# A hybrid recurrent decoder step on one core: the RWKV-7 scan in three products per chunk

## The chip, the cores and the metric

One Trainium2 chip, of which one core is used. The metric is the device time of one execution in microseconds (us). An execution computes one step of a two-layer decoder trunk for 512 prompt rows and 8 x 4 sample rows, 544 columns in all.

## The reference

```python
# layer 0: RG-LRU and RWKV-7 side by side; layer 1: HGRN2; a SwiGLU FFN after each, RMSNorm everywhere
p = rmsnorm(x) @ w_in_ab                     # 1024 -> 1024 (RG-LRU) + 1792 (RWKV-7)
m = pf + (shifted - pf) * mu                 # r, k, v and three low-rank inputs
decay = exp(-exp(-softplus(-(w0 + tanh(xw) @ w2)) - 0.5));  a = sigmoid(a0 + xa @ a2)
kk = (k * k_k) / |k * k_k|;  k = k * (1 + (a - 1) * k_a)
def _rwkv_step(S, inp):                      # 8 heads, S is 64 x 64 [value, key]
    sk = einsum('bhvk,bhk->bhv', S, kk_t)
    S = S * w_t - sk (kk_t * a_t) + v_t k_t
    return S, einsum('bhvk,bhk->bhv', S, r_t)
y = concat(gelu(gate) * rg_lru(conv(u)), (groupnorm(o) + bonus) * g) @ w_out_ab
```

The outputs are y for both groups and all the new states, in float32.

## The kernel before

Everything lies transposed: features on partitions, the 544 columns along the free dimension. A projection (`dense_steps`) makes one block of 128 outputs in two halves of 272 columns; each half is 24 matmuls (8 blocks of the inner dimension, each as high times high, high times low, low times high in fp32r). A block is called a column here: 48 matmuls, two weight loads of 256 KB on SP's queue, a rounding of each on ScalarE (wh, L198) and a difference on VectorE or GpSimd (wl, L201). Three wh and three wl buffers hold weights. The result is taken from its bank by VectorE (X, L465), and `proj_end` mixes it with its shifted self (d on GpSimd, L471; then L473).

The RWKV-7 recurrence is done in chunks of 32 steps, 16 chunks, 8 heads. Heads are numbered by p (0 to 3, a block of 128 features) and par (which half of the block). `mixer0` stages it:

1. **Projections ahead**: the low-rank block and k blocks.
2. **Features** (`FEAT` lists the steps): `front` normalises kappa, `back` makes the decay products eb, KB (key and kappa parts divided by the decay, 64 columns a chunk) and A (kappa times decay), `couple` multiplies A with KB to get the coupling of the steps of a chunk (NTt, and masked into AN), `alphas` transposes A into AN on TensorE.
3. **Inverse**: the coupling goes through DRAM (nd_p) to a layout of 128 (head, chunk) pairs; VectorE inverts the two diagonal 16 x 16 blocks of each 32 x 32 triangle in 15 steps (L670, L672); ScalarE transposes (Zc); both go through DRAM (y_p, z_p) to Yt and Zt.
4. **Fixed order** (`MID` lists the steps): a and b start a half of a `keys`, r a `receptance`, v is a value projection, g the gate's; capitals are their second parts (transposes into TM, `scores` and bonus), x a transpose of values to DRAM (vT). From here on `in_order = "all"`: every matmul of the steps waits for the one before it in program order.
5. **Scan**: `PLAN` interleaves the chunks (c), the sample group's steps (s), group norms (g, h) and the output projection's start (l). `join` completes the inverse of four chunks (32 x 32 tiles), `fold` multiplies AN by it on TensorE and copies the result to wa. Then for each chunk a first product (wa with Z, where Z holds the 64 state rows, the values and the corrections of a chunk), two copies into Z, and a second product (TM with Z) to which the decayed state is added for the next Z; `outputs` reads Z too. Between the products `fill(n)` issues n matmuls of the RG-LRU branch's projections; `HOP` gives the two counts.

What no fixed order binds is placed by a planner at build time, which simulates the queues with its own costs; `high_priority` moves work ahead. All DMAs are issued on SP's queue in order. The engines run their queues in order.

The lines that matter in profiles: L167 all matmuls of `mm`, known by tile (acc projections, scps scores, wyps fold, ch the two products, ops outputs, jps join, knps and kkps the kappa norm, sps the sample's corrections); L596 to L599 the kappa product and its small copies; L612 the mask of AN; L670, L672 inverse; L686 loads of Yt and Zt; L730 r times decay; L784 and L782 copies of the first product (and of wa); L788 the load of values; L861 the decayed state; L876 the next state.

## Time and profile before

| | us |
|---|---|
| median of three runs | 1554.47 (1553.48 to 1555.07) |
| the profiled execution | 1550.75 |
| its span, first to last instruction | 1549.0 |
| TensorE busy in the span | 1475.5 (95%) |
| VectorE busy | 841.7 (54%) |
| ScalarE busy | 565.9 (37%) |
| GpSimd busy | 422.2 (27%) |

The profile is one execution. Busy times of stretches give engines in the order TensorE, its weight loads, VectorE, ScalarE, GpSimd, then the granted TensorE clock as a share of full speed, the share of the DMA engines and GB/s. A row of a group has the line, the engine, the operation, output<-inputs, shapes and count, then busy us and mean ns of one, then the idle time just before with what ended it. A row of a timeline has start, length, engine, line, operation. A row of the chain of waits has start, length and what held the end. Matmuls overlap, so a mean of one is a latency; the pace is read from many in a row. A matmul in float32 shows as two instructions.

The mixer of layer 0 takes the first 351 us; the features lie at about 59 to 105, the fixed order at 105 to 182, the chunks at 195 to 336.

### The profile page before, as it was taken

Reading aid. Unit: us, or ns where it says so; the run is one execution under the profiler, and the core shown is the slowest. Engines: PE = TensorE matmul, PEld = TensorE weight load, DVE = VectorE, ACT = ScalarE, POOL = GpSimd, SP = SyncE. Lnnn points to the kernel's source line nnn. Section 1 sums busy time; section 2 is a strip of 40 time slices with the busy share of each in tenths; the row PEclk is TensorE's granted clock in tenths of the full one; section 3 lists DMA queues with packets and bytes.
Section 4 is the critical chain, followed back from the end, with each engine's and each line's share of the span. In section 5 each row is a group of like instructions: output and inputs, shape, how many; then the busy total and the mean of one; then the engine's idle time right before and its main releaser. Section 6 shows DMA issues by size and latency. Waiting matters only on the chain.

```text
span 1549.0 us, 33454 instructions
## 1 busy us (share of the span) xinstructions
PE 1475.5 (95%) x13888; PEld 1425.7 (92%) x13888; DVE 841.7 (54%) x1560; ACT 565.9 (37%) x1030; POOL 422.2 (27%) x545
## 2 busy tenths in 40 slices
PE   6669999879999999999999999999999999999997
PEld 6658888759999999999999999999999999999997
DVE  7646535785544344434576767666674443444444
ACT  5644234473433223222353333333453322332224
POOL 4535624553111011001124434444431100110010
PEclk9869988889999999999999999999999999999999
DMA  4115401122222322322231222322332223223221
GB/s 160 52 31 137 124 25 34 43 94 87 82 95 84 90 89 89 90 83 95 81 122 67 85 85 86 101 96 84 103 123 89 95 81 92 89 89 89 83 75 59
DMA packets 91480, 133.79 MB, mean 86 GB/s; under 512 B 28448, under 2 KB 34336, under 8 KB 91200
## 3 DMA queue, kind: packets, MB, share of 16 engines
q1 hardware_dynamic: 91328, 131.65, 27.2%
q8 instruction: 109, 1.79, 0.5%
q14 instruction: 43, 0.35, 0.1%
HBM read 120.60 MB, written 11.02 MB: 85 GB/s over the span
## 4 chain that ended last, share of the span: by engine, by line
PE 85%; DVE 6%; ACT 3%; issue 2%; DMA 2%; POOL 1%; SPq 0%; DVEq 0%; POOLq 0%; ACTq 0%
PE acc L167 74%; PE lv L167 2%; PE ops L167 1%; PE wyps L167 1%; PE ch L167 1%; DMA wd<-down 1%; PE ds L167 0%; POOL wl L201 0%; PE tr L1528 0%; PE nps L167 0%; PE scps L167 0%; DVE Pd L670 0%; DVE cf L1038 0%; DVE Y L672 0%; PE opsm L167 0%
## 5 line engine op out<-in xcount | busy, mean ns | idle before, releaser
L167 PE MATMUL acc<-xg,wh 128*128 128x272 f32 x4544 | 881.8, 292 | 13.5 <-ACT xg L258 6.5
L167 PEld LDWEIGHTS acc<-xg,wh 128*128 128x128 f32 x4544 | 718.2, 190 | 21.4 <-ACT xg L258 6.5
L167 PE MATMUL acc<-xg,wl 128*128 128x272 f32 x2272 | 651.2, 292 | 1.1 <-DVE wl L201 0.7
L198 ACT ACTIVATE wh<-wf 128x512 fp32r<-128x512 f32 (+1 forms) x404 | 250.7, 621 | 632.0 <-PE acc L167 538.3
L167 PEld LDWEIGHTS acc<-xg,wl 128*128 128x128 f32 x2272 | 427.4, 190 | 5.0 <-DVE wl L201 1.4
L201 DVE TENSOR_TENSOR wl<-wf,wh 128x512 fp32r<-128x512 f32 (+1 forms) x373 | 266.7, 716 | 190.1 <-ACT wh L198 164.0
L1232 POOL TENSOR_TENSOR S<-S,rstd 128x272 f32<-128x272 f32 x88 | 74.5, 847 | 645.6 <-ACT S L1231 645.6
L167 PE MATMUL acc<-h,wh 128*128 128x272 f32 x1280 | 236.9, 288 | 0.0
L167 PEld LDWEIGHTS acc<-h,wh 128*128 128x128 f32 x1280 | 198.0, 188 | 0.0
L167 PE MATMUL acc<-h,wl 128*128 128x272 f32 x640 | 176.7, 287 | 0.0
L167 PEld LDWEIGHTS acc<-h,wl 128*128 128x128 f32 x640 | 118.1, 188 | 0.0
L1235 DVE TENSOR_TENSOR hh<-acc,S 128x272 f32<-128x272 f32 x88 | 38.9, 442 | 125.6 <-PE acc L167 123.8
L167 PE MATMUL acc<-cat,wh 128*128 128x272 f32 (+2 forms) x512 | 99.4, 294 | 5.1 <-ACT wh L198 5.1
L167 PEld LDWEIGHTS acc<-cat,wh 128*128 128x128 f32 x512 | 82.2, 193 | 5.7 <-ACT wh L198 5.3
L1231 ACT ACTIVATE S<-t 128x272 f32<-128x272 f32 x88 | 37.8, 431 | 124.0 <-DVE t L1230 124.0
L1252 DVE TENSOR_TENSOR x<-acc,x 128x272 f32<-128x272 f32 x80 | 35.1, 439 | 83.5 <-PE acc L167 83.1
L167 PE MATMUL acc<-cat,wl 128*128 128x272 f32 (+2 forms) x256 | 73.8, 295 | 3.9 <-POOL wl L201 3.9
L1230 DVE TENSOR_TENSOR t<-acc,rstd 128x272 f32<-128x272 f32 x88 | 38.8, 442 | 71.2 <-PE acc L167 71.1
L276 POOL TENSOR_TENSOR ssq<-ssq,sq 128x544 f32<-128x544 f32 x33 | 46.6, 1411 | 87.7 <-ACT sq L275 87.3
L1502 POOL TENSOR_TENSOR K<-K,G 128x256 f32<-128x256 f32 (+1 forms) x48 | 39.6, 824 | 77.5 <-PE lv L167 77.5
L167 PEld LDWEIGHTS acc<-cat,wl 128*128 128x128 f32 x256 | 48.7, 192 | 4.5 <-POOL wl L201 4.5
L201 POOL TENSOR_TENSOR wl<-wf,wh 128x512 fp32r<-128x512 f32 x31 | 42.6, 1378 | 25.9 <-ACT wh L198 24.0
(355 smaller groups left out, 1549.6 us busy)
## 6 DMA issues: line engine op xcount, KB each, us to landing
wf<-gate SPq DMA_DIRECT2D x88, 256.0 KB, 2.6
wf<-up SPq DMA_DIRECT2D x88, 256.0 KB, 2.7
wf<-down SPq DMA_DIRECT2D x72, 256.0 KB, 2.7
wf<-w_in_c SPq DMA_DIRECT2D x64, 256.0 KB, 2.5
wf<-w_in_ab SPq DMA_DIRECT2D x44, 256.0 KB, 2.7
x<-xT SPq DMA_DIRECT2D x16, 272.0 KB, 4.4
wf<-w_out_ab SPq DMA_DIRECT2D x16, 256.0 KB, 2.5
S<-hS SPq DMA_DIRECT2D x8, 512.0 KB, 3.8
```

The costliest lines, as they stand in the source:

```text
L167: return self.seq(self.nc.tensor.matmul(out, lhsT, rhs, start=start, stop=stop, skip_group_check=True), chain)
L198: nc.scalar.activation(wh[:, :n], wf[:, :n], AF.Copy)
L201: eng.tensor_tensor(wl[:, :n], wf[:, :n], wh[:, :n].bitcast(F32), OP.subtract)
L276: eng.tensor_tensor(self.ssq, self.ssq, t, OP.add)
L1230: nc.vector.tensor_tensor(t[:, c], ps, rs()[:, c], OP.mult)
L1231: nc.scalar.activation(S[:, c], t[:, c], AF.Silu)
L1232: nc.gpsimd.tensor_tensor(S[:, c], S[:, c], rs()[:, c], OP.mult)
L1235: nc.vector.tensor_tensor(hh[:, c], ps, S[:, c], OP.mult)
L1252: nc.vector.tensor_tensor(x[:, c], ps, x[:, c], OP.add)
L1502: PTT(kv[:, :, 0], kv[:, :, 0], g2[:, :, 1, None].to_broadcast([128, m, b]), OP.mult)
```

## The change

The first product of a chunk is split. Before, the inverse was folded into the kappa rows ahead of the chunks (fold, 16 matmul calls for two chunks at a time) and one product gave the corrections. Now the first product gives the right-hand side (kappa rows with Z) in quarter q of the partitions for each head pair, VectorE copies it (rhs), a second product multiplies it by the inverse, with the heads on the four diagonal 32 x 32 quarters of the array, four copies on VectorE put the corrections into Z, and the state's product follows. `HOP` has three counts.

For that the rows of kappa, r and the scores share one array W (64 columns a chunk: 32 for kappa, 32 for r, the sample as chunk 16), so `scores` makes both masked parts in one matmul a chunk, in three tiles; the order of corrections and values in Z's rows and in KB's columns depends on p's parity (`quad`, VS, US). AN, A2, As, Ws, tmask, `alphas` and `fold` go. `couple` handles two p at once with half the columns, and writes nd_p in eight DMAs of 32 partitions; Yt and Zt are loaded in 16 DMAs instead of 8; the values of a chunk in four DMAs instead of two. The pools of W and TM are part of m0, the inverse's tiles are opened after the features, and the scan's pool follows where eb and KB lay.

The value projections stand first in `MID`, and the fixed order begins only at the step r3, so that v0 to v3, a3 and b3, a1 and A3 are placed by the planner.

```diff
--- before.py
+++ after.py
+FREE = 'r3'
-MID = 'a3 v0 A3 b3 v2 B3 a1 v3 A1 b1 r3 B1 a2 v1 R3 A2 b2 r0 x B2 x a0 r1 x R0 A0 x b0 r2 x R1 B0 g R2'
+MID = 'v0 v2 v3 a3 v1 A3 b3 a1 r3 B3 A1 b1 a2 r0 R3 B1 A2 x b2 a0 x r1 x B2 R0 A0 x b0 r2 x R1 B0 g R2'
-FEAT = 'f0 b0 f2 f1 b1 b2 f3 n0 n1 b3 n2 n3'
+FEAT = 'f0 b0 f2 f1 b1 b2 n0 f3 b3 n1'
-HOP = (11, 11)
+HOP = (8, 7, 7)
...
-        AN = m0.tile([128, 4, 4, 256], F32, name="AN")
-        nc.gpsimd.memset(AN[:, :, :, 96:192], 0.0)
+        W = [[m0.tile([128, NC1, 64], F32, name=f"W{par}{p}") for p in range(4)] for par in range(2)]
+        TM = [m0.tile([128, NC1, 64], F32, name=f"TM{p}") for p in range(4)]
...
-        v_rows = (slice(64, 96), slice(0, 32))
-        s_rows = (slice(96, 128), slice(32, 64))
+        VS, US = [slice(CH, 64), slice(0, CH)] * 2, [slice(0, CH), slice(CH, 64)] * 2
+        def quad(par, e):
+            return slice(64 - 64 * par + 32 * e, 96 - 64 * par + 32 * e)
...
         def scores(p):
-            ps = mps("scps").rearrange("p (c t) -> p c t", t=CH)
-            for c in range(NCH):
+            for c0, cn in ((0, 8), (8, 8), (16, 1)):
+                ps = self.ms.tile([128, 8, 64], F32, tag="m", name="scps")
+                for c in range(c0, c0 + cn):
+                    for par in range(2):
+                        r = par_rows[par]
+                        self.mm(ps[sc_rows[par], c - c0], KB[p][r, c], W[par][p][r, c])
                 for par in range(2):
-                    r = par_rows[par]
-                    self.mm(ps[sc_rows[par], c], KB[p][r, c], W[par][r, c, p])
-            for par in range(2):
-                sr = sc_rows[par]
-                TT(W[par][sr, :, p], ps[sr], smask[sr, 0, None, CH:].to_broadcast([64, NCH, CH]), OP.mult)
...
-        def alphas(p):
-            ps = mps("atps").rearrange("p (g k) -> p g k", k=128)
-            for g in range(4):
-                nc.tensor.transpose(ps[:, g], A2[p][:, 4 * g:4 * g + 4].rearrange("p c t -> p (c t)"), ident)
-            an = AN[:, :, p]
-            out = bass.AP(tensor=an.tensor, offset=an.offset, ap=[an.ap[0], an.ap[1], [192, 2], [1, 64]])
-            ACT(out, ps.rearrange("p g (q k) -> p g q k", q=2), AF.Copy)
+                    sr = sc_rows[par]
+                    TT(W[par][p][sr, c0:c0 + cn], ps[sr, 0:cn],
+                       smask[sr, p % 2, c0 // 16, None, :].to_broadcast([64, cn, 64]), OP.mult)
...
-            STT(KB[p][:, :, CH:], chunks(ta), -0.5, chunks(emb), op0=OP.mult, op1=OP.mult)
-            al = A2[p]
-            E(f"al{p % 2}")(al, chunks(kap), chunks(eb[p][:, 0:NT]), OP.mult)
-            nc.gpsimd.tensor_copy(al[:, 0:NCH, 0:1], kap[:, 0:SEQ:CH][:, :, None])
-            nc.gpsimd.tensor_copy(al[:, NCH, 0:CH:NS], kap[:, SEQ::NS])
-            nc.gpsimd.tensor_copy(As[:, p], al[:, NCH])
-
-        def couple(p):
-            ps = [self.ms.tile([128, 4, 64], F32, tag="m", name="ndps") for _ in range(2)]
+            STT(KB[p][:, :, US[p]], chunks(ta), -0.5, chunks(emb), op0=OP.mult, op1=OP.mult)
+            for par in range(2):
+                r = par_rows[par]
+                al = W[par][p][r, :, 0:CH]
+                E(f"al{par}")(al, chunks(kap[r]), chunks(eb[p][r, 0:NT]), OP.mult)
+                nc.gpsimd.tensor_copy(al[:, 0:NCH, 0:1], kap[r, 0:SEQ:CH][:, :, None])
+                nc.gpsimd.tensor_copy(al[:, NCH, 0:CH:NS], kap[r, SEQ::NS])
+
+        def couple(s):
+            ps = mps("ndps").rearrange("p (c t) -> p c t", t=CH)
             for c in range(NCH):
+                for e in range(2):
+                    p = 2 * s + e
+                    for par in range(2):
+                        r = par_rows[par]
+                        self.mm(ps[quad(par, e), c], W[par][p][r, c, 0:CH], KB[p][r, c, US[p]])
+            ACT(NTt[:, s], ps, AF.Copy)
+            for q in range(4):
+                r = slice(32 * q, 32 * q + 32)
+                nc.sync.dma_start(nd_p[4 * s + q].rearrange("c t i -> t c i"), NTt[r, s])
-                    self.mm(ps[par][quarter(c), c // 4], A2[p][r, c], KB[p][r, c])
-            for par in range(2):
-                nt = NTt[:, :, 4 * par + p]
-                ACT(nt, ps[par][:, :, CH:], AF.Copy)
-                nc.sync.dma_start(nd_p[4 * par + p].rearrange("(g c) t i -> (c t) g i", c=4), nt)
-            for par in range(2):
-                TT(AN[:, :, p, 64 + 64 * par:96 + 64 * par], ps[par][:, :, 0:CH],
-                   tmask[:, None, :].to_broadcast([128, 4, CH]), OP.mult)
...
-                alphas(p)
...
-        wt = self.open("wt")
-        W = [wt.tile([128, NCH, 4, CH], F32, name=f"W{par}") for par in range(2)]
-        Ws = [wt.tile([128, 4, 64], F32, name=f"Ws{par}") for par in range(2)]
-        TM = [wt.tile([128, NC1, 64], F32, name=f"TM{p}") for p in range(4)]
+        iv = self.open("inv", side="right")
...
-            for g in range(4):
+            for h in range(8):
+                r = slice(32 * (h % 4), 32 * (h % 4) + 32)
                 for zt, dr in ((Yt, y_p), (Zt, z_p)):
-                    nc.sync.dma_start(zt[:, g], dr.rearrange("h (g c) i t -> g (c i) h t", c=4)[g])
+                    nc.sync.dma_start(zt[r, :, h // 4], dr[h].rearrange("c i t -> i c t"))
...
-                E(f"w{par}")(W[par][r, :, p], chunks(rm[r, :SEQ]), chunks(eb[p][r, 1:1 + SEQ]), OP.mult)
-                nc.gpsimd.tensor_tensor(Ws[par][r, p, CH:], rm[r, SEQ:], eb[p][r, 1 + SEQ:], OP.mult)
+                E(f"w{par}")(W[par][p][r, :, CH:], chunks(rm[r]), chunks(eb[p][r, 1:]), OP.mult)
...
-        self.in_order = "all"
         parts = {}
         values = values_out()
         for e in MID.split():
+            if e == FREE:
+                self.in_order = "all"
...
-        both = chp.tile([128, 2, 4, 64], F32, name="ch")
-        chain = [both[:, i] for i in range(2)]
+        chain = chp.tile([128, 512], F32, name="ch")
+        cr, cu = (chain[:, 128 * i:128 * i + 128].rearrange("p (s v) -> p s v", v=64) for i in range(2))
+        cs = chain[:, 256:512].rearrange("p (a v) -> p a v", v=64)
...
         def load_v(c, zc):
             for par in range(2):
-                nc.sync.dma_start(zc[par][v_rows[par]], vT[CH * c:CH * c + CH, :, par_rows[par]])
-
+                for e in range(2):
+                    nc.sync.dma_start(zc[par][quad(par, 1 - e), e::2], vT[CH * c:CH * c + CH, e::2, par_rows[par]])
+        heads = [(p, par) for p in range(4) for par in range(2)]
...
+            ps = ms.tile([128, 4, 2, HB], F32, tag="m", name="jps")
+            for s in range(2):
+                for c in range(4 * g, 4 * g + 4):
+                    for q in (slice(32 * i, 32 * i + 32) for i in range(4)):
+                        if part:
+                            self.mm(ps[q, c % 4, s], Zt[q, c, s], joined[g][q, c % 4, s])
+                        else:
+                            self.mm(ps[q, c % 4, s], NTt[q, s, c], Yt[q, c, s, HB:])
...
-        def fold(g, cs):
-            pss = [self.acc.tile([128, 2, 4, CH], F32, tag="acc", name="wyps", bufs=3) for _ in cs]
-            for par in range(2):
-                for p in range(4):
-                    for ps, c in zip(pss, cs):
-                        q = quarter(c)
-                        self.mm(ps[:, par, p], AN[q, g, p, 128 * par:128 * par + 128],
-                                Yt[q, g, 4 * par + p], chain=True)
-            for ps, c in zip(pss, cs):
-                wa = z.tile([128, 2, 4, CH], F32, tag="wa", name="wa", bufs=6)
-                copy(c % 2, wa, ps)
-                folded[4 * g + c] = wa
...
-                    self.mm(ops[quarter(p), c % 4, par], W[par][:, c, p], zc[par][:, p], chain=True)
+                    self.mm(ops[quarter(p), c % 4, par], W[par][p][:, c, CH:], zc[par][:, p], chain=True)
...
-            with first():
-                fold(0, (0, 1))
-                fold(0, (2, 3))
             for c in range(NCH):
+                rhs = z.tile([128, 2, 64], F32, tag="rhs", name="rhs", bufs=2)
                 with first():
-                    for p in range(4):
-                        for par in range(2):
-                            self.mm(chain[0][s_rows[par], p], folded[c][:, par, p], zc[par][:, p], chain=True)
-                    for par in range(2):
-                        copy(par, zc[par][s_rows[par]], chain[0][s_rows[par]])
+                    for p, par in heads:
+                        self.mm(cr[quad(par, p % 2), p // 2], W[par][p][:, c, 0:CH], zc[par][:, p], chain=True)
+                    nc.vector.tensor_copy(rhs, cr)
...
-                if c < 12:
-                    with first():
-                        if c % 4 > 1:
-                            fold(c // 4 + 1, ((0, 1), (2, 3))[c % 2])
-                        else:
-                            join(c // 4 + 1, c % 4)
+                    if c < 12 and c % 4 < 2:
+                        join(c // 4 + 1, c % 4)
                 self.fill(HOP[0])
                 with first():
-                    for p in range(4):
+                    for p, par in heads:
+                        q = quad(par, p % 2)
+                        self.mm(cu[q, p // 2], Yt[q, c, p // 2], rhs[q, p // 2], chain=True)
+                    for e in range(2):
                         for par in range(2):
-                            sr = sc_rows[par]
-                            self.mm(chain[1][par_rows[par], p], TM[p][sr, c], zc[par][sr, p], chain=True)
+                            q = quad(par, e)
+                            nc.vector.tensor_copy(zc[par][q, e::2], cu[q])
+                self.fill(HOP[1])
+                with first():
+                    for p, par in heads:
+                        sr = sc_rows[par]
+                        self.mm(cs[par_rows[par], p], TM[p][sr, c], zc[par][sr, p], chain=True)
                     for par in range(2):
                         r = par_rows[par]
-                        TT(zn[par][r], chain[1][r], sp[r], OP.add)
+                        TT(zn[par][r], cs[r], sp[r], OP.add)
...
-                self.fill(HOP[1])
+                self.fill(HOP[2])
                 yield
```

More of the change, by code (lines that the diff above doesn't have):

```diff
@@ L106, in rows, with pair @@
         return np.concatenate([top, bot, top, bot], 0)
-    c["smask"] = np.stack([rows(strict, incl), rows(strict * same, incl * same)], 1)
-    c["tmask"] = np.tile(strict.T, (4, 1))
+    def pair(flip):
+        m = np.stack([rows(strict, incl), rows(strict * same, incl * same)], 1)
+        return m.reshape(2, 2, 32, 2, 64)[:, ::-1].reshape(128, 2, 64) if flip else m
+    c["smask"] = np.stack([pair(True), pair(False)], 1)
     c["upper"] = np.tile((np.arange(CH) < CH // 2)[:, None], (4, 1)).astype(np.float32)
@@ L504, in mixer0 @@
         L = f.tile([128, NT], F32, name="L")
-        A2 = [f.tile([128, NC1, CH], F32, name=f"A2{p}") for p in range(4)]
-        As = m0.tile([128, 4, CH], F32, name="As")
         def tmp(name, bufs=2):
@@ L614, in couple @@
[L614 to L621 removed]
+                    self.mm(ps[q_rows[par]], KB[p][r, NCH, US[p]], W[par][p][r, NCH, 0:CH])
@@ L623, in mixer0 @@
+                ACT(ss, ps, AF.Copy)
+                for par in range(2):
+                    nc.sync.dma_start(nd_s[4 * par + p], ss[q_rows[par]])
         kaps = [None] * 4
@@ L985, in sample @@
                 for p in range(4):
-                    self.mm(sps[s_rows[par], p], Yts[q_rows[par], p], rhs[q_rows[par], p])
-                ACT(zc[par][s_rows[par]], sps[s_rows[par]], AF.Copy)
+                    self.mm(sps[quad(par, p % 2), p], Yts[q_rows[par], p], rhs[q_rows[par], p])
+                for e in range(2):
+                    ACT(zc[par][quad(par, e), e::2], sps[quad(par, e), e::2], AF.Copy)
             yield
@@ L1136, in mixer0 @@
         nc.sync.dma_start(self.o["h_o"], h_sb)
-        self.close("rg", "scan", "wt", "m0", "ms_s", "ops0", "chain")
+        self.close("rg", "scan", "m0", "ms_s", "ops0", "chain")
         self.ms = self.open("ms", bufs=4, space=PSUM)
```

53 lines of the change are left out of this document (14 added, 39 removed).

## The prediction

> **What bounds the kernel now.** I read first the chain of waits of the page, then busy times by stretch, the acc groups of one stretch, and the timelines of TensorE (PE) and SyncE's queue (SPq) around the seams.
>
> ```profile
> PE 85%; DVE 6%; ACT 3%; issue 2%; DMA 2%; POOL 1%; SPq 0%; DVEq 0%; POOLq 0%; ACTq 0%
> ```
> ```profile
> core 0: us, PE busy (x) PEld busy (x) DVE busy (x) ACT busy (x) POOL busy (x), PEclk, DMA share, GB/s
> 59.50:105.00 45.50, 20.62 (x347) 15.52 (x346) 27.83 (x42) 21.90 (x45) 19.45 (x30) 0.64 0.10 22
> 128.00:182.00 54.00, 50.65 (x590) 48.06 (x588) 31.05 (x58) 21.60 (x45) 34.69 (x61) 1.00 0.50 133
> 195.40:240.80 45.40, 41.68 (x778) 36.93 (x776) 20.63 (x46) 17.42 (x30) 14.75 (x22) 0.88 0.12 33
> 283.80:330.50 46.70, 41.43 (x479) 34.09 (x479) 37.06 (x79) 23.64 (x43) 28.94 (x31) 0.89 0.16 51
> ```
>
> TensorE sets the end nearly everywhere, but the change touches only the first 351 us, and there the share hides two limits. In 59.5 to 105 (the features) TensorE works 20.6 of 45.5 us at a granted clock of 0.64: it waits for short vector steps. From 105 to 182 (the phase in fixed order) it is full. In the scan it is nearly full until about 284; after that VectorE is busy 79% of the time.
>
> ```profile
> L167 PE MATMUL acc<-xg,wl x1: 375/375/375, 59.3 to 59.3; 128*128 128x272 f32 x1
> ```
> ```profile
> L167 PE MATMUL acc<-xg,wh 128*128 128x272 f32 x276 | 53.5, 292 | 1.8 <-ACT wh L198 1.8
> L167 PE MATMUL acc<-xg,wl 128*128 128x272 f32 x138 | 40.1, 291 | 1.1 <-DVE wl L201 0.7 <-POOL wl L201 0.4
> ```
> ```profile
> 148.19 5.98 PE acc L167 x48
> ```
>
> The first row holds the only projection matmul in the features. The second pair is 105 to 182: 414 matmuls, eight columns of 48 and the 30 of the first fill. The order has nine columns (four v, four r, the gate), so v0 ran before 59.5 and v1, v2, v3 stand after 105, although they need only xg and weights: A3 stands ahead of v2 in the fixed order, and A3 needs KB3, one of the last products of the features. A column costs 5.98 us.
>
> **Value projections.** Put outside the order, v1 to v3 can fill the 24.9 idle us: 3 x 5.98 = **-17.9** from the full stretch. Each brings vector work into the features.
>
> ```profile
> L201 DVE TENSOR_TENSOR wl<-wf,wh 128x512 fp32r<-128x512 f32 x84 | 61.3, 731 | 50.2 <-ACT wh L198 44.0 <-PE acc L167 2.9
> L465 DVE TENSOR_TENSOR X<-acc,rstd 128x272 f32<-128x272 f32 x28 | 11.8, 435 | 7.3 <-PE acc L167 5.3 <-ACT rstd L308 1.9
> L473 DVE SCALAR_TENSOR_TENSOR v<-d,vec,X 128x544 f32<-128x544 f32 x4 | 3.1, 779 | 0.4 <-POOL d L472 0.4
> L596 DVE TENSOR_TENSOR A<-kap,eb 128x544 f32<-128x544 f32 x2 | 1.4, 725 | 1.4 <-ACT eb L584 1.4
> L612 DVE TENSOR_TENSOR AN<-ndps,tmask 128x128 f32<-128x128 f32 x8 | 1.9, 284 | 4.4 <-ACT NTt L609 4.4
> L596 POOL TENSOR_TENSOR A<-kap,eb 128x544 f32<-128x544 f32 x2 | 2.7, 1344 | 0.0
> L598 POOL COPY A<-kap 128x8 f32<-128x8 f32 x4 | 2.0, 499 | 0.0
> L471 POOL TENSOR_TENSOR d<-X 128x544 f32<-128x544 f32 x14 | 17.4, 1242 | 0.0
> ```
>
> VectorE: 6 x 0.435 + 4 wl x 0.731 (a third goes to POOL) + 3 x 0.779 = 7.9. The kappa product is now one VectorE and one POOL instruction of 64 partitions for each p instead of one of either: +2 x 0.725, and the eight masks of AN go, -2.3. Together +7.0 on an engine with 17.7 us idle. POOL takes three d (3.7), two more kappa products (2.7) and about four more small copies net (2.0) into 26 idle us. The chain here alternates between engines, so an added operation costs only where it stands ahead of a due one: bounds 0 and 7.0, I take **+3**.
>
> Against this stands the clock. The same eight matmuls take
>
> ```profile
> 48.53 0.93 PE knps L167 x8
> 65.62 2.18 PE knps L167 x8
> 84.24 2.18 PE knps L167 x8
> ```
>
> before and inside the features, twice on the chain: **-2.5** if the columns keep the clock up, else 0. The 16 transposes of alphas and their copies also go; I count nothing, since vector steps set this stretch. Were they bare, it would be about another microsecond for each p.
>
> **Scores, couple, inverse.**
> ```profile
> 137.04 2.05 PE L167 MATMUL scps<-W,KB 64*64 64x32 f32 x64 [1.32 <-POOL W L730]
> ```
>
> Scores keep their number of matmuls, with 64 columns moving instead of 32 and three tiles to mask instead of two: between nothing and 0.65 us per r (2.05 for 64 now; 2.7 at the pace of the 64x64 products below, 16 in 0.68). I take **+1** for all four. The added masks lie beside projections. POOL's product of r with eb must precede each scores; one stall of 1.32 is there today, and the cover stays one column: **+1**, bounds 0 and 4. Couple does the same number of matmuls with half the columns and its first half moves ahead of f3: 0, hidden by vector steps as above.
>
> ```profile
> 127.40 0.22 DVE Pd L670
> ```
> ```profile
> 130.50 2.93 SPq L686 DMA_DIRECT2D Yt<-y_p  x4
> 133.53 2.52 SPq L686 DMA_DIRECT2D Zt<-z_p  x4
> ```
> ```profile
> 182.03 0.73 PE L167 MATMUL jps<-Yt,NTt 32*32 32x16 f32 x64
> ```
>
> The inverse ends at 127.6, its loads are issued by 136 and wanted at 182. After: nd_p is still eight DMAs, now bunched four by four (about 2 us later), and Yt and Zt take 16 issues in place of 8; at 2.93/4 each that is at most 6 us more on SPq, ahead of weight loads. The loads land near 147; the first join would come near 167. I count **0**, covered by the r projections; without the cover, a microsecond for each that they are late. The scan's tiles now lie where eb and KB were, so Z's first writes wait for r2's product; the gate's column (5.98) stands behind that one, and without it up to the 4.14 of a Z load (below) would be bare.
>
> Features and fixed order: -17.9 + 3 - 2.5 + 1 + 1 = **-15**.
>
> **Start of the scan.**
>
> ```profile
> 186.25 1.33 PE L167 MATMUL wyps<-Yt,AN 32*128 32x32 f32 x12
> 188.31 2.34 PE L167 MATMUL wyps<-Yt,AN 32*128 32x32 f32 x20 [0.72 <-issue]
> 191.81 3.62 PE L167 MATMUL wyps<-Yt,AN 32*128 32x32 f32 x32 [1.16 <-DVE wa L784]
> ```
> ```profile
> 181.88 4.14 DMA Z<-vT
> ```
> ```profile
> L788 SPq DMA_DIRECT2D Z<-vT x18: 538/548/690, 181.1 to 236.4; - x18
> ```
>
> The first fold stands bare from 186.25 to 195.4 (191.81 + 3.62), its second half behind a copy that VectorE does late. Without a fold the first product can go at once: -9.1. It needs its values, landed at 186.0 with no slack now. Each slot takes four DMAs instead of two, the sample's too: four more issues of 0.55 ahead of the first slot's last, +2.2. **-7**, bounds -9 and -3.
>
> **Each chunk.**
>
> ```profile
> 204.53 0.66 PE L167 MATMUL ch<-Z,wa 128*32 128x64 f32 x15
> 207.00 0.41 PE L167 MATMUL acc<-xg,wh 128*128 128x272 f32 x2
> 207.34 0.68 PE L167 MATMUL ch<-Z,TM 64*64 64x64 f32 x16
> 207.95 0.43 PE L167 MATMUL ops<-Z,W 128*32 128x64 f32 x16
> 211.58 1.97 PE L167 MATMUL wyps<-Yt,AN 32*128 32x32 f32 x32
> 238.28 1.06 PE L167 MATMUL sps<-rhss,Yts 32*32 32x64 f32 x8
> 284.71 3.93 PE L167 MATMUL wyps<-Yt,AN 32*128 32x32 f32 x32
> ```
> ```profile
> L876 DVE TENSOR_TENSOR Z<-ch,sp 64x256 f32<-64x256 f32 x32 | 13.5, 421 | 14.0 <-PE ch L167 9.0 <-ACT gg L1074 2.2 <-ACT wh L198 1.9
> L784 DVE COPY Z<-ch 32x256 f32<-32x256 f32 x16 | 6.9, 430 | 12.9 <-PE ch L167 12.6
> ```
>
> TensorE: six folds go (five like 1.97, one of 3.93): -13.7. The first product uses four column groups instead of two, as ops does: 0.66 to 0.43, -3.7 over 16 (bounds 0 and -3.7). The new product of 32x32 tiles isn't in the trace in this arrangement: below, ops with 0.43; above, two of sps, whose eight share one tile, 2.1. Here neighbours never share a tile, as in ops and in jps (64 in 0.73): 0.45, +7.2 (bounds 6.9 and 34, for the range half of that). Sum -10.2; the 22 fills a chunk stay.
>
> Latency: the copy of rhs (128 elements a partition, as L612: 0.28) hides under eight fill matmuls (8 x 0.125). Behind the new product stand four copies, 4 x 0.28 and a start of 0.15 = 1.27, against seven fills, 0.88: bare 0.4 in each chunk, **+7** with the gaps between copies. Behind the waiting state's product queue, in order, the outputs, the fill, the sample's products and the next chunk; the two sums into the next slot wait for it. VectorE gets 5 x 0.28 and loses one Z copy (0.43) and half a copy of a fold, of the same size (0.21): +0.76 a chunk. Up to 284 it is idle enough; in the 5.5 chunks at 79% I take it whole: **+4.2** (bounds 0 and 12). ScalarE loses its copies, which bounds nothing.
>
> Loop: -10.2 + 7 + 4.2 = **+1**, bounds -8 and +20.
>
> The Trainium skill, TensorEngine Tiling (Array Packing), Key Properties, says that a change of tiling mode drains the engine, which speaks against one more product between fills. In the rows at 207 the 64x64 product starts about 0.09 us later than another matmul of the fill would have, so two more changes in 16 chunks would add 2.9 us, and the whole would come to -18.
>
> **Sum.** -15 - 7 + 1 = -21. The profiled execution took 1550.75 (span 1549.0): 1529.7. The median shown, 1554.47, lies 3.7 higher, so on its scale **1533**.
>
> **Rivals.** *More moves.* The order now begins at r3, and nothing precedes r3's matmuls: 24.9 idle us hold a fourth column. Against it: r3's buffers and the planner. Another -6, with no stretch of the features -3 more, and -2 in the loop: 1522.
>
> *They don't move.* Three weight buffers and in-order ACT and DVE queues may keep the columns behind the features, or they stretch that chain as much as they free. For it: the chain there lives on DVE and ACT, as the columns do; against: 17.7 idle us. Features and order give -1, the rest -6: 1547.
>
> *The third hop decides (slower).* Place: VectorE's queue in the scan. Both new waits are on VectorE, whose other operations, 0.4 to 0.8 us in the rows above, run to their end. If each of the two waits for one like L473 (0.78), a chunk gets 1.56 us longer, 25 in all: -21 + 25 = +4, 1558. It decides from 21/16 = 1.3 us a chunk. For it: 79% busy after 284, and a fold's copy is late behind VectorE at 191.8; against: half idle until 284, and a hop to ScalarE goes.
>
> **Chances.** Forecast 0.47, more moves 0.20, not moved 0.16, third hop 0.17. A measurement here tells 0.2% (3 us) from nothing. Of "not moved" 0.03 and of the third hop 0.02 fall within that: faster 0.80, same 0.05, slower 0.15. The forecast's own range is 1522 to 1545; with the bounds above and most of the rivals, 1511 to 1555.
>
> **What would show it.** Right: some 140 acc matmuls between 59 and 105 at a clock near 1; the first join near 167; under 1.5 us from the new product to the state's product; no wyps. Wrong: features ending after 110, join waiting for Yt, chunks over 9 us, TensorE idle behind the four copies for more than a microsecond.

## The result, and the profile after

The changed kernel takes **1541.53 us** (median of four runs, 1540.40 to 1541.86) against 1553.97 (1549.24 to 1555.07) for the kernel before on the same chip: a ratio of 0.9924, 95% interval 0.9903 to 0.9946. That is 12.4 us by medians; the profiled executions, 1550.75 and 1541.22, lie 9.5 apart, and the sum of the prediction (-21) is made on that scale; less than half of it came. One of the four runs with the fills on VectorE below was in the slow state (1789 us) and is left out of its figures.

The chain of waits of the page after is almost the one before:

```profile
PE 84%; DVE 7%; ACT 3%; issue 2%; DMA 2%; POOL 1%; SPq 1%; DVEq 0%; POOLq 0%; ACTq 0%
```

Busy times by stretch, in the columns of the prediction, with the seams where this trace has them:

```profile
59.50:107.00 47.50, 40.33 (x532) 35.44 (x530) 40.34 (x53) 24.66 (x44) 32.86 (x48) 0.92 0.19 57
107.00:128.00 21.00, 11.22 (x74) 10.20 (x73) 13.19 (x35) 6.27 (x17) 9.20 (x16) 0.61 0.23 55
128.00:176.00 48.00, 42.30 (x526) 39.00 (x526) 30.41 (x59) 18.58 (x40) 24.21 (x44) 0.93 0.44 116
```

The features, 20.6 us of TensorE work at a clock of 0.64 before, are now nearly full: 40.33 of 47.5 us at 0.92. The hole has moved. It stands now in the first 21 us of the fixed order, where TensorE works 11.22 us at 0.61; before, the same length of this phase was full (20.11 us from 105 to 126, at 0.97).

The table puts seams of several kernels side by side; the runs are those of the next section. Each is read from TensorE's timeline: the end of the last couple's product (ndps), the first join (jps), the first product of chunks 0, 1 and 15, and the first product of the norm that follows the mixer (nps). What lies behind nps takes 1145 to 1146 us in all of them. The first product of the kappa norm (kkps), ahead of all these seams, starts at 43.1 to 44.9 us, so a difference of under 2 us in the place of a single seam says nothing; lengths between seams repeat better.

| us | features end | fixed order, to first join | to chunk 0 | chunks 0 to 15 (to the start of 15) | to nps | idle TensorE in the fixed order |
|---|---|---|---|---|---|---|
| before | 104.0 | 78.0, to 182.0 | 13.3 | 134.5 | 73.2 | 4.2 |
| after | 107.0 | 68.8, to 175.8 | 4.2 | 141.8 | 72.1 | 15.5 |
| projections back | 102.1 | 91.6, to 193.8 | 4.2 | 139.8 | 73.5 | 14.7 |
| r0 early | 109.5 | 66.7, to 176.2 | 4.2 | 143.1 | 75.1 | 16.8 |
| fills on VectorE | 104.5 | 68.3, to 172.8 | 4.2 | 141.8 | 73.4 | 13.9 |
| state first | 106.4 | 69.0, to 175.5 | 4.2 | 137.0 | 72.5 | 16.0 |
| two hops | 104.4 | 69.3, to 173.7 | 4.5 | 124.5 | 72.4 | 16.2 |
| before, no folds | 103.2 | 79.0, to 182.2 | 13.3 | 121.8 | 76.8 | 3.0 |
| projections back, two waits out | 100.8 | 85.6, to 186.4 | 4.2 | 141.1 | 71.6 | 10.5 |
| split copies | 106.5 | 69.1, to 175.6 | 4.2 | 158.7 | 75.8 | 16.0 |
| fills ahead | 104.8 | 67.6, to 172.4 | 4.3 | 141.2 | 73.5 | 13.3 |
| four edits | 105.8 | 82.2, to 188.0 | 4.2 | 135.6 | 73.4 | 27.0 |
| projections back, fills ahead | 101.4 | 84.8, to 186.1 | 4.2 | 141.7 | 72.5 | 9.7 |
| fills ahead, no inverse steps | 107.7 | 60.7, to 168.3 | 4.2 | 141.1 | 73.5 | 7.8 |

So from before to after the first join comes 6.2 us earlier, the way from it to chunk 0 is 9.1 shorter, the chunks are 7.3 longer and the rest 1.1 shorter: 9.1 in all. (Counted from the first kkps, at 43.5 before and 44.7 after, the first join comes 7.4 us earlier.) The gain that the value projections promised is the first of these, and most of it is missing. The groups of waits on TensorE's timeline after say where:

```profile
114.39 1.12 PE L687 MATMUL tmps<-ident,KH 128*128 128x128 f32 x4 [7.37 <-POOL KH L678]
116.89 1.12 PE L687 MATMUL tmps<-ident,KH 128*128 128x128 f32 x4 [1.38 <-POOL KH L678]
119.25 1.11 PE L687 MATMUL tmps<-ident,KH 128*128 128x128 f32 x4 [1.04 <-POOL KH L678]
134.55 1.09 PE L687 MATMUL tmps<-ident,KH 128*128 128x128 f32 x4 [3.58 <-DVE W L528]
136.67 0.40 PE L693 MATMUL tmps<-ident,KHs 128*64 128x128 f32 x1 [1.02 <-DVE W L528]
...
179.99 0.43 PE L171 MATMUL ch<-Z,W 128*32 128x64 f32 x16
...
191.20 1.65 PE L171 MATMUL rpss<-S,am 64*32 64x64 f32 x32 [3.69 <-DMA S<-rS]
```

Idle time before an instruction stands in brackets with what ended it. Five transposes of the keys wait, together 14.4 us: three for the scaled keys (KH, made by GpSimd), two for VectorE's masks of the first scores. The first product of chunk 0 goes at 179.99 in 0.43 us, as forecast; in that chunk TensorE then waits 3.69 us for the sample group's state.

### The profile page after: what moved, and what is told of

Its sections match the earlier page's. It is cut to its first block, busy times and chain, and to the rows that moved or that the text cites. A ratio compares the mean times of both kernels' runs of the same rounds, so it can differ in the third digit from the quotient of the medians.

```text
span 1539.4 us, 33537 instructions
## 1 busy us (share of the span) xinstructions
PE 1465.2 (95%) x13872; PEld 1408.7 (92%) x13872; DVE 860.2 (56%) x1618; ACT 552.5 (36%) x997; POOL 418.3 (27%) x540
## 4 chain that ended last, share of the span: by engine, by line
PE 84%; DVE 7%; ACT 3%; issue 2%; DMA 2%; POOL 1%; SPq 1%; DVEq 0%; POOLq 0%; ACTq 0%
PE acc L171 74%; PE lv L171 2%; PE ops L171 1%; PE ch L171 1%; DVE Z L842 1%; DVE t L571 0%; PE ds L171 0%; PE tr L1503 0%; DVE W L528 0%; PE nps L171 0%; DVE wl L205 0%; DMA S<-rS 0%; DMA x<-xT 0%; DMA wd<-down 0%; DVE Pd L653 0%
```

## The experiments

**Projections back.** The old fixed order with the rest of the change kept.

```diff
-FREE = 'r3'
-MID = 'v0 v2 v3 a3 v1 A3 b3 a1 r3 B3 A1 b1 a2 r0 R3 B1 A2 ...'
+FREE = 'a3'
+MID = 'a3 v0 A3 b3 v2 B3 a1 v3 A1 b1 r3 B1 a2 v1 R3 A2 b2 r0 ...'
```

> Undoes one part alone: the old list of steps with all of them in fixed order (v0 first, v2 after A3, v3 after B3, v1 after a2); scan, arrays and DMAs stay as changed. Theory: the value projections gave only some 6 us in the features and fixed order, because the keys' transposes they had covered became bare (TensorE idle for 12.9 us between 107 and 120, against 4 us in the whole phase before); the start of the scan gives 9, the sample's state load and the hops take back 7. So this kernel takes about 1541 + 6 = 1547, with TensorE idle before the first tmps of 2 us at most. Rival: the projections gave the full 18 us and the three hops lost it again; then this kernel is slower than the one before, about 1559.

Measured: 1558.99 us (1557.67 to 1562.21), ratio 1.005 (1.0032 to 1.0068): the rival's number. Moving the projections is worth 18.0 us at the first join (193.8 to 175.8), and the rest of the change, which I had at about nothing here, costs 11.8 (182.0 to 193.8); counted from the first kkps these are 18.1 and 10.7. Its two long waits on TensorE, and what SyncE's queue held ahead of the second:

```profile
109.33 1.11 PE L687 MATMUL tmps<-ident,KH 128*128 128x128 f32 x4 [7.22 <-POOL KH L678]
140.53 0.82 PE L171 MATMUL acc<-xg,wh 128*128 128x272 f32 x2 [6.07 <-ACT wh L202]
```
```profile
126.42 2.50 SPq L670 DMA_DIRECT2D Yt<-y_p  x4
...
136.37 21.90 SPq L201 DMA_DIRECT2D wf<-w_in_ab  x7
```

The weights were issued only when the last of the sixteen loads of Yt and Zt was out, 10 us after the first.

**r0 early.** The second r projection right behind the first, where the features could still hold it.

```diff
-MID = '... a1 r3 B3 A1 b1 a2 r0 R3 B1 ...'
+MID = '... a1 r3 r0 B3 A1 b1 a2 R3 B1 ...'
```

> The changed kernel with one step moved: r0 stands right behind r3, ahead of B3 and A1, so that its 48 matmuls are there when the keys' transposes wait for GpSimd's KH. Theory (bare transposes): about one column, 5 us, is won: 1536, and the idle time of TensorE between 107 and 120 falls from 12.9 to about 7. Rival (the phase is bound by VectorE's and GpSimd's chain anyway, KH, masks, r times decay): within 1.5 us of 1541, the idle time only moves to a later place.

Measured: 1540.38 (1538.76 to 1545.95), ratio 0.9933 (0.9913 to 0.9953): no gain. The features grew by 2.5 us, the fixed order shrank by 2.1, and its idle time was 16.8 us, no less than after the change. (The trace is of its slowest execution, 1545.95.) The same two kinds of wait stand there; the first is shorter, and two later ones are longer, 2.51 us instead of 1.04 for the third scaled keys and 2.88 instead of 1.02 for the second wait on the masks:

```profile
117.38 1.11 PE L687 MATMUL tmps<-ident,KH 128*128 128x128 f32 x4 [4.53 <-POOL KH L678]
...
132.66 0.63 PE L687 MATMUL tmps<-ident,KH 128*128 128x128 f32 x4 [3.59 <-DVE W L528]
```

**Fills on VectorE.** The inverse's arrays are filled with zeros and ones on VectorE.

```diff
-            nc.gpsimd.memset(zero, 0.0)
+            nc.vector.memset(zero, 0.0)
...
-                nc.gpsimd.memset(y, 0.0)
+                nc.vector.memset(y, 0.0)
```

> The changed kernel with the four fills of the inverse's tiles (zero, Y, Y4) on VectorE instead of GpSimd. Their space was the features', so they wait for the last nd_s write (112.1), and on GpSimd the first KH stood behind them for 4.3 us. Theory (GpSimd's queue holds KH): KH starts near 108, the first transposes near 109.5 instead of 114.4, and 3 to 4 us are won: 1537.5. Rival (something else holds the phase): the transposes come earlier, the first join does not; within 1.5 us of 1541.

Measured: 1540.38 (1539.64 to 1541.60), ratio 0.9930 (0.9905 to 0.9954): no gain. The first wait falls, two others grow:

```profile
106.35 1.12 PE L687 MATMUL tmps<-ident,KH 128*128 128x128 f32 x4 [1.83 <-POOL KH L678]
...
114.44 1.11 PE L687 MATMUL tmps<-ident,KH 128*128 128x128 f32 x4 [4.40 <-POOL KH L678]
131.41 1.09 PE L687 MATMUL tmps<-ident,KH 128*128 128x128 f32 x4 [4.31 <-DVE W L528]
```

**State first.** The sample group's state is loaded ahead of the first chunks' values.

```diff
-            nc.sync.dma_start(S0, I["rS"])
+            with tc.high_priority(offset=2 * CHAIN_PRIO):
+                nc.sync.dma_start(S0, I["rS"])
```

> The changed kernel with the 1 MB load of the sample's states ahead of the scan's value loads on SyncE's queue. Theory: the doubled value loads (16 issues from 172 to 184) pushed it to 184.6, its 6.4 us end at 191, and the sample's first product, in fixed order, held TensorE 3.7 us inside chunk 0 (12.9 us instead of 9.1 before). Then about 3.5 us are won: 1538. Rival: the values of chunk 0 then come late by as much, and the start of the scan loses what chunk 0 wins: within 1.5 us of 1541.

Measured: **1536.61** (1531.15 to 1538.03), ratio 0.9898 (0.9871 to 0.9925), 4.9 us under the changed kernel. The two intervals overlap, but the seam agrees: chunks 0 to 15 fall from 141.8 to 137.0. SyncE's queue in the kernel before, where the planner had put the state ahead of all the values, in the changed kernel and in this run:

```profile
178.93 0.38 SPq L939 DMA_DIRECT2D S<-rS  x1
...
181.09 7.93 SPq L788 DMA_DIRECT2D Z<-vT  x8
```
```profile
172.34 11.57 SPq L774 DMA_DIRECT2D Z<-vT  x16
...
184.64 0.36 SPq L913 DMA_DIRECT2D S<-rS  x1
```
```profile
171.95 0.68 SPq L774 DMA_DIRECT2D Z<-vT  x1
172.74 0.51 SPq L914 DMA_DIRECT2D S<-rS  x1
173.29 10.38 SPq L774 DMA_DIRECT2D Z<-vT  x15
```

**Two hops.** The changed kernel without the product with the inverse.

```diff
-                    nc.vector.tensor_copy(rhs, cr)
+                    for e in range(2):
+                        for par in range(2):
+                            q = quad(par, e)
+                            nc.vector.tensor_copy(zc[par][q, e::2], cr[q])
...
-                        self.mm(cu[q, p // 2], Yt[q, c, p // 2], rhs[q, p // 2], chain=True)
```

> The changed kernel without the product with the inverse: the four copies go straight from the first product's result to Z. It leaves out the 128x128 copy of the right-hand side and the 16 instructions of the product with Yt in each chunk of the prefill scan (so the recurrence is not the reference's); the fill between the hops stays. Theory (TensorE's own work sets a chunk): 16 chunks lose 0.43 us each, c0 to c15 shrink by 6.9 us, about 1534.5 us. Rival (the hop's latency sets it): product, copy and the waits between go too, 0.43 + 0.29 + about 0.3 for the hand-overs = 1.0 us a chunk, 16 us in all, about 1525.5 us. A third case, that fill covers the hop: within 2 us of the changed kernel, 1540 to 1543.

Measured: 1521.96 (1521.65 to 1524.55), ratio 0.9813 (0.9798 to 0.9827). Chunks 0 to 15 take 124.5 instead of 141.8: the third hop costs 17.3 us, 1.1 a chunk, of which TensorE's work is 0.43. The rival is nearest: the hop costs far more than its product, in spite of the fill. TensorE's waits for the chain's copies fall from 16.9 to 9.2 us in the 16 chunks, and its busy time falls by 13.2: the product itself (6.8), and most of the rest is that the same projection matmuls take 87.8 instead of 93.2 us.

**Before, no folds.** The kernel before without the folds in its loop.

```diff
-                        if c % 4 > 1:
-                            fold(c // 4 + 1, ((0, 1), (2, 3))[c % 2])
-                        else:
+                        if c % 4 < 2:
                             join(c // 4 + 1, c % 4)
...
-folded[c][:, par, p]
+folded[c % 4][:, par, p]
```

> The kernel before with the six folds inside the scan's loop left out: the state's product of chunks 4 to 15 reads the folded keys of chunks 0 to 3 (so its output is not the reference's); the joins stay. Theory (my term: each fold's products cost their TensorE time in full, 13.7 us): c0 to c15 shrink from 134.5 to about 121 us, about 1540 us. Rival (the folds ran where TensorE waited for the chain's copies): c0 to c15 shrink by under 4 us, 1550 us or above.

Measured: 1542.35 (1541.96 to 1544.57), ratio 0.9944 (0.9929 to 0.9958). Chunks 0 to 15 shrink by 12.7 us (134.5 to 121.8), about what the folds' own time is; 3.6 us come back in the stretch behind chunk 15. Why that is longer I did not follow up.

**Projections back, two waits out.** The run with the old order, with fills on VectorE, and the sixteen loads outside the part that is moved ahead.

```diff
-            nc.gpsimd.memset(zero, 0.0)
+            nc.vector.memset(zero, 0.0)
...
-                nc.gpsimd.memset(y, 0.0)
+                nc.vector.memset(y, 0.0)
...
-            for h in range(8):
-                r = slice(32 * (h % 4), 32 * (h % 4) + 32)
...
+        for h in range(8):
+            r = slice(32 * (h % 4), 32 * (h % 4) + 32)
```

> The kernel with the projections back in the old fixed order (1559 us, +13.6 us in the fixed order against the kernel before), with two waits taken out: the three fills of the inverse's arrays on VectorE instead of GpSimd, so that the scaled keys are not queued behind them (7.2 us of idle TensorE), and the sixteen loads of Yt and Zt issued behind the weights' loads on SyncE's queue (6.1 us of idle TensorE before the first product of a weight block). Theory (these two waits, and some 2 us of lowered clock behind each, are the 13.6 us that the rest of the change costs in the fixed order): the fixed order falls from 91.6 to 79 us and the time to about 1546 us. Rival (what costs is the wider scores, three PSUM tiles and six masks for each of four groups, which these edits leave): the waits move elsewhere, the fixed order stays above 87 us, about 1556 us.

Measured: 1552.68 (1548.01 to 1554.58), ratio 1.0001 (0.9989 to 1.0013). Half-way: 7.4 of the 11.8 us at the first join are back (1.5 of them lie ahead of the first kkps). The weights' wait is gone. In its place TensorE stands before a weight block's low part, which VectorE makes:

```profile
117.59 0.60 PE L171 MATMUL acc<-xg,wl 128*128 128x272 f32 x1 [6.62 <-DVE wl L205]
```

**Split copies.** The run with the state first, and two of the four copies into Z on ScalarE.

```diff
-                            nc.vector.tensor_copy(zc[par][q, e::2], cu[q])
+                            copy(par, zc[par][q, e::2], cu[q])
```

> The changed kernel with the sample state's load first (1536.6 us), and the four copies from the product with the inverse to Z split: two on VectorE and two on ScalarE (before the change ScalarE had copies of this hop). Theory (the hop from the new product to the state's product is on the path, four copies in a row of 0.29 us each): 0.57 us less in each of 16 chunks, 9 us at most, about 1529 us. Rival (the fill between covers the four copies, waits come from what stands ahead of them on the engine, and ScalarE has its own queue): within 3 us, 1534 to 1539.

Measured: 1561.78 (1560.94 to 1563.92), ratio 1.0068 (1.0053 to 1.0083): 25 us slower than without the split. Both theories missed. One chunk, TensorE and then ScalarE:

```profile
246.59 1.12 PE L171 MATMUL ch<-Z,TM 64*64 64x64 f32 x16 [2.42 <-ACT Z L767]
```
```profile
243.49 0.27 ACT L767 ACTIVATE Z<-ch 32x128 f32<-32x128 f32 x1 [3.06 <-DVE Z L769]
243.67 0.61 ACT L202 ACTIVATE wh<-wf 128x512 fp32r<-128x512 f32 x1
244.30 1.28 ACT L1050 ACT_TABLE_LOAD   x1
245.59 0.66 ACT L1050 ACTIVATE gg<-gg 128x544 f32<-128x544 f32 x1
246.27 0.27 ACT L767 ACTIVATE Z<-ch 32x128 f32<-32x128 f32 x1
```

Between the two copies of one hop ScalarE's queue holds 2.6 us of the other branch's work, 1.28 of it the load of a function table. VectorE needs 1.19 us for four copies in a row. In the 16 chunks TensorE waits 33.2 us for these copies, against 15.3 without the split.

**Fills ahead.** Y, Y4 and the zeros on storage that is free from the start, filled before the features.

```diff
+        Y = TM[0][:, 0:NCH].rearrange("p c t -> p (c t)").rearrange("p (i t) -> p i t", t=CH)
+        Y4 = TM[2][0:64, 8, 0:16].rearrange("p (i t) -> p i t", t=NS)
+        zero = TM[2][0:32, 0:4].rearrange("p c t -> p (c t)").rearrange("p (h t) -> p h t", t=CH)
+        nc.gpsimd.memset(zero, 0.0)
...
         f2 = self.open("feat2")
...
-            Y = iv.tile([128, CH, CH], F32, name="Y")
```

> The changed kernel with one thing changed: the inverse's arrays that are filled beforehand (Y, Y4 and the zeros) lie in the storage of the transposed keys TM0 and TM2, which is free until those are written, and are filled before the features. In the changed kernel they lie on storage that the features give back, so GpSimd's fills wait for the features' last transfer, and the scaled keys are queued behind them (7.4 us of idle TensorE). Theory (that hand-over of storage is the largest of the new waits in the fixed order): the fixed order falls from 68.8 to about 60 us (7.4 us and some 2 us at a lowered clock behind it), the time to about 1532 us. Rival (as with the fills on VectorE, the next wait takes its place, because the fixed order hangs on the masks and the one buffer of the scaled keys): the fixed order stays above 67 us, about 1540 us.

Measured: 1538.50 (1537.64 to 1544.03), ratio 0.9932 (0.9909 to 0.9955), not told from the changed kernel's 0.9924. The first wait is gone here too (1.84), and again the masks' wait is longer, 6.05 instead of 3.58. TensorE, then VectorE, then ScalarE:

```profile
130.54 1.08 PE L687 MATMUL tmps<-ident,KH 128*128 128x128 f32 x4 [6.05 <-DVE W L535]
```
```profile
113.47 0.21 DVE L653 TENSOR_TENSOR Pd<-TM,Ns 128x30 f32<-128x30 f32 x1 [5.54 <-DMA Ns<-nd_s]
...
125.47 0.21 DVE L655 TENSOR_TENSOR TM<-TM,Pd 128x30 f32<-128x30 f32 x1
...
128.28 0.69 DVE L205 TENSOR_TENSOR wl<-wf,wh 128x512 fp32r<-128x512 f32 x1 [2.25 <-ACT wh L202]
129.00 1.39 DVE L535 TENSOR_TENSOR W<-scps,smask 64x512 f32<-64x512 f32 x2
```

```profile
125.77 1.96 ACT L656 ACTIVATE Zc<-TM 128x1024 f32<-128x1024 f32 x1 [5.43 <-DVE TM L655]
127.63 0.62 ACT L202 ACTIVATE wh<-wf 128x512 fp32r<-128x512 f32 x1
```

From 113.5 to 125.7 VectorE works off the inverse, and the masks come behind it, but not at once: VectorE then waits 2.25 us. ScalarE's transposing copy Zc needs the inverse's last step; the rounding of a weight block (wh) stands behind Zc on ScalarE's queue; VectorE's wl needs that wh; and the masks stand behind wl. This way from the inverse's end to the masks takes 3.3 us.

**Four edits.** Fills ahead, state first, two buffers for the scaled keys, and each scores just ahead of a projection.

```diff
-MID = '... r3 B3 A1 b1 a2 r0 R3 B1 A2 x b2 a0 x r1 x B2 R0 A0 ...'
+MID = '... r3 B3 A1 R3 r0 b1 a2 B1 A2 x b2 a0 x R0 r1 B2 A0 ...'
...
-KH = ph.tile([128, 8, 64], F32, tag="KH", name="KH")
+KH = ph.tile([128, 8, 64], F32, tag="KH", name="KH", bufs=2)
```

> The changed kernel with four edits: fills ahead of the features, sample state's load first, two buffers for the scaled keys, and each scores moved to stand just ahead of a projection in the fixed order, so that TensorE works on the projection's own banks while VectorE masks. Theory (the waits add up): 1541.5 - 4.9 (state first) - 9 (fills) - 3.6 - 1.4 - 1.0 - 1.0 (masks and key buffer) = about 1521 us, idle TensorE in the fixed order under 5 us. Rival (the fixed order ends with a vector chain of r2, its scores and the gate, which no reordering shortens): 1541.5 - 4.9 and little else, about 1534 us.

Measured: 1548.91 (1546.96 to 1550.23), ratio 0.9987 (0.9976 to 0.9999). Both missed. The keys' and masks' waits are short, but the scores now wait for their own projection's vector work, 11.90, 5.18 and 4.96 us; the first of these:

```profile
138.80 3.89 PE L171 MATMUL scps<-W,KB 64*64 64x64 f32 x68 [11.90 <-POOL X L467]
```

In the changed kernel a whole projection stands between an r and its scores. I had taken that cover away: 22 us.

**Projections back, fills ahead.** The old order with fills ahead and the sixteen loads behind.

```diff
-FREE = 'r3'
+FREE = 'a3'
...
+        Y = TM[0][:, 0:NCH].rearrange("p c t -> p (c t)").rearrange("p (i t) -> p i t", t=CH)
...
-            for h in range(8):
+        for h in range(8):
```

> The kernel with the projections in the old fixed order (1559 us), fills ahead of the features as in the run with that name, and the sixteen loads of Yt and Zt behind the weights' loads. Theory (the inverse's place on the features' storage and the sixteen loads are the whole 13.6 us that the rest of the change costs in the fixed order; with the fills on VectorE the first of them only changed its engine): the fixed order falls from 85.6, as it was with the fills on VectorE, to 79 us, idle TensorE under 6 us, time about 1546 us. Rival (the wider scores cost the rest): the fixed order stays above 84 us and the time above 1550 us.

Measured: 1551.16 (1548.98 to 1553.73), ratio 0.9994 (0.9982 to 1.0005); the fixed order 84.8 us. The rival's numbers, but not its reason: the wait is the one seen with the fills on VectorE, and VectorE is again in the inverse, which began at 109.7 while the low part was made at 117.2. That is 9.6 us after its high part (107.61); in the kernel before, with the same order of steps, the low part stood earlier among the inverse's steps, 3.6 us after the high part (110.61 and 114.25). The place is the planner's, and no run fixes it.

```profile
117.96 0.60 PE L171 MATMUL acc<-xg,wl 128*128 128x272 f32 x1 [6.46 <-DVE wl L205]
```
```profile
109.74 0.21 DVE L653 TENSOR_TENSOR Pd<-TM,Ns 128x30 f32<-128x30 f32 x1 [10.81 <-ACT wh L202]
...
117.22 0.68 DVE L205 TENSOR_TENSOR wl<-wf,wh 128x512 fp32r<-128x512 f32 x1
```

**Fills ahead, no inverse steps.** So the last run takes the inverse's steps off VectorE.

```diff
-            for i in range(HB - 1):
+            for i in range(0):
...
-            for i in range(NS - 1):
+            for i in range(0):
```

> The run with the fills ahead (1538.5 us), without the inverse's recurrence on VectorE: the loops of Pd and Y (30 instructions on 128 partitions, 6 on 64) are left out, so Y stays the identity and the outputs are not the reference's; everything that is loaded and stored around it stays. Theory (since the value projections have left the fixed order, nothing covers these 12 us of VectorE, which run from 113.5 to 125.7; the masks of the first scores stand behind them, at 129.0, and TensorE waits 6.05 + 1.03 us for the bank they hold): both waits go, and the lowered clock behind them, the fixed order falls from 67.6 to 58 to 60 us, the time to about 1530 us. Rival (TensorE waits for the scaled keys' one buffer, the weights or r0, and the masks are only named because they end last): the fixed order stays above 65 us, 1536 us or above.

Measured: 1532.60 (1528.53 to 1534.09), ratio 0.9872 (0.9852 to 0.9893), 5.9 us under the run with the steps, and the intervals don't overlap. The fixed order falls from 67.6 to 60.7, its idle time from 13.3 to 7.8; the 6.05 is gone and 1.32 is left of the masks' waits:

```profile
129.04 0.27 PE L693 MATMUL tmps<-ident,KHs 128*64 128x128 f32 x1 [1.32 <-DVE W L535]
```

One thing more went with the steps: Y is constant then, so its store and the eight loads of Yt were issued before the features. And ScalarE's Zc, which needs Y, ran at 108.30, so the wh of that weight block went at 124.00, the wl at 124.66 and the masks at 125.39. So the run takes the inverse out of the masks' way, but does not part VectorE's busy time from Zc's place ahead of the wh, nor either from SyncE's queue; a run with the wh ahead of Zc would, and was not made.

## Why the prediction was right and where it was wrong

The forecast was 1533, faster, with a range of 1511 to 1555; 1541.5 lies in it. That owes something to the width of the range: of the 21 us on the profiled scale 9.5 came, because two terms below were some 9 and 6 us too good, and one 2 us too bad. By the parts of the sum:

**Value projections, -17.9 + 3 - 2.5: right in size, in part by luck.** 18.0 us at the first join, but as the sum of two misses: the fixed order is 22.8 shorter, not 17.9, and the features 4.9 longer, not 0.5. 196 of their matmuls now lie in the features, where I expected some 140: r3 went with v1 to v3, as the rival "more moves" had it.

```profile
L171 PE MATMUL acc<-xg,wh 128*128 128x272 f32 x130 | 25.9, 293 | 0.0
L171 PE MATMUL acc<-xg,wl 128*128 128x272 f32 x66 | 19.3, 293 | 0.0
```

So the fourth column bought nothing like that rival's 6 us: the features grew by nearly as much. And of the two slow kappa products only one became fast, 1.09 us (the 0.93 of the prediction's row was only a piece of the chain):

```profile
89.27 2.15 PE L171 MATMUL knps<-kn,spread 128*128 128x136 f32 x8 [2.52 <-DVE kn L548]
```

**Scores, couple, inverse, +2 and 0: the step that failed.** I wrote of the inverse "I count 0, covered by the r projections" and looked only at when Yt and Zt are wanted. With the old order this part costs 11.8 us, by three things of which I had seen one. The inverse's tiles are opened on storage that the features give back, so GpSimd's fills wait for the features' last transfer with the scaled keys behind them (7.22, and 7.37 in the changed kernel, whose GpSimd is below); this stood in the change. Sixteen loads on SyncE's queue hold back the weights (6.07); I had given the loads up to 6 us on that queue and called it covered. And VectorE's 12 us of inverse had a cover: the value projections, which ask 2.6 us of VectorE for a column of 6 by the prediction's own sum (7.9 for three). The move that won 18 us took it away. After it, the first scores fall into those 12 us, and their masks stand behind the inverse, Zc, wh and wl as in the run with the fills ahead (GpSimd, then VectorE):

```profile
112.09 0.30 POOL L635 MEMSET zero<- 32x256 f32 x1 [4.28 <-DMA nd_s<-ss]
```
```profile
117.34 0.20 DVE L653 TENSOR_TENSOR Pd<-Y,Ns 128x30 f32<-128x30 f32 x1
...
129.44 0.21 DVE L655 TENSOR_TENSOR Y<-Y,Pd 128x30 f32<-128x30 f32 x1
...
132.29 0.69 DVE L205 TENSOR_TENSOR wl<-wf,wh 128x512 fp32r<-128x512 f32 x1 [2.30 <-ACT wh L202]
133.02 1.39 DVE L528 TENSOR_TENSOR W<-scps,smask 64x512 f32<-64x512 f32 x2
```

That removing one of these waits lets the next grow is shown by four runs (r0 early, fills on VectorE, fills ahead, and the old order with two waits out); that the inverse, by way of Zc, is the last of them, by the run without its steps, but for the earlier loads of Yt there. Which part of the 11.8 us in the old order belongs to which of the three is not settled: with two removed, 4.1 to 4.4 us and a wait of 6.5 remain, although the cover is back; one thing that differs there from the kernel before is the place of the weights' low part among the inverse's steps. The stall of r before its scores, +1 with "the cover stays one column", held (the changed kernel has no such wait), and the run with four edits shows the price without it.

**Start of the scan, -7: -9.1 measured.** The fold's 9.1 are all won; the four more value loads, +2.2, don't stand there.

**Loop, +1: +7.3 measured.** The terms held. The folds, -13.7, were worth 12.7. The product with the inverse takes 0.43 (forecast 0.45) and the copies 0.29 each:

```profile
248.72 0.42 PE L171 MATMUL acc<-xg,wh 128*128 128x272 f32 x2
249.06 0.43 PE L171 MATMUL ch<-rhs,Yt 32*32 32x64 f32 x16
249.42 0.39 PE L171 MATMUL acc<-xg,wl 128*128 128x272 f32 x1
```

For the whole hop I had 7.2 + 7 + 4.2 = 18.4 and the run without it gives 17.3. With -3.7 for the first product, -12.7 - 3.7 + 17.3 makes +0.9, and with the state first the loop stands at +2.5 (137.0 against 134.5). TensorE's own sums agree: between these two its work in the chunks falls by 9.0 us (forecast 10.2) and its idle time grows by 11.4 (forecast 7 + 4.2). But the wait is not the even 0.4 a chunk of the forecast. In the changed kernel eleven chunks wait for the four copies, 13.9 us in all, six of them for over a microsecond, the longest for 3.4. Of the signs of being wrong this one came true, and so did chunks over 9 us (9.5 in the mean; 9.0 before).

The other 4.8 us are the late load of the sample's state: the value loads' +2.2 was put at the right queue and at the wrong waiter, since I asked what the first chunk waits for and not what is queued behind its loads. Twice the loads were not all of it: before, the state's load stood ahead of the values, and the planner had now put it behind sixteen of them. TensorE's idle time in the chunks is 24.3 us with the late load and 24.0 without; what falls is its busy time, 117.4 to 112.9, at a granted clock of 0.88 and 0.91.

The Trainium skill, TensorEngine Tiling (Array Packing), Key Properties, says that a change of tiling mode drains the engine. The rows above agree with the size taken from the trace of before: a pair of fill matmuls is followed by the next after 0.25 us, by the 32x32 product after 0.34, so 0.09 for a change.

**The rivals.** "They don't move" fell with the 196 matmuls, and "third hop decides" with the run of two hops: 1.1 us a chunk in all, product included, where it needed 1.3 beyond my sum.

The fastest version that leaves nothing out is the changed one with the sample's state loaded first: 1536.61, ratio 0.9898, though its interval overlaps that of the changed kernel.

## What to carry to other kernels

When work is moved out of a full phase to fill a hole, ask what it was covering there: the long vector job beside it becomes the next bound, also by way of another engine's queue (a copy that needs its result, with the weights' rounding behind it), and removing one wait ahead of it only lengthens the next. A tile pool that is opened later inherits the last reader of the storage it gets, and with it every instruction queued behind the first write to it. For each DMA that is added, look for what is issued behind it, not only for who waits for its data, and whether the planner has moved something there.

## What the runs showed of the hardware

After the 7.37 us of idle time TensorE was slow for longer than the wait itself suggests: four transposes took 1.12 us instead of 0.60, and pairs of projection matmuls followed at 0.45 us and not 0.25 until 123.3, 4 us after steady work began at 119.25. In the run with the projections back the slow pace lasted from 109.33 to 115.0, 5.7 us.

```profile
120.85 0.66 PE L171 MATMUL acc<-xg,wh 128*128 128x272 f32 x2
...
123.44 0.41 PE L171 MATMUL acc<-xg,wh 128*128 128x272 f32 x2
...
146.60 0.60 PE L687 MATMUL tmps<-ident,KH 128*128 128x128 f32 x4
```

The Trainium skill, TensorE: Matmul & The Clock Gate, Part 1, has half rate after at least one idle window of about 3.4 us and full rate after at least one busy window of that length; these rows agree. So each long wait in the fixed order cost, as an estimate from these rows (4 to 5.7 us at about half the pace), some 2 to 3 us more than its own length.

The other surprise was ScalarE: its 0.27 us copy is as short as VectorE's 0.29, and still moving half the copies there cost 25 us, because its queue holds longer work of another branch, in the rows above 2.6 us with a table load of 1.28 us in it.
